# Half of a long convolution on VectorE, two taps a pass on TensorE, modulations turned in one piece, grouped heads' scores in F32

## The chip, the core and the metric

One NeuronCore of a Trainium2 chip runs the whole program. The metric is the device time of one execution in microseconds (us). Engines: PE is TensorE (PEld its weight loads), DVE VectorE, ACT ScalarE, POOL GpSimd, SP SyncE, which here only issues DMAs.

## The reference

One step of a two-layer diffusion backbone in F32, width 1024, on 128 context tokens and 512 latent tokens, which the program keeps side by side as 640 columns. Layer 0 mixes with convolutions, layer 1 with attention; each is followed by a SwiGLU network of width 2816. Cut to what the change touches:

```
m = silu(cvec) @ ada_w[l] + ada_b[l]              # 6 modulation vectors, for context and latents
h = rmsnorm(x) * (1 + scale) + shift
# layer 0
gate_b, gate_c, xa, ub = split(h @ w_in)
ya = gate_b * depthwise_conv(gate_c * xa, sc_w)   # 3 taps
z  = (ub + b)[:, :512] * sigmoid((ub + b)[:, 512:])
z  = depthwise_conv(z, cf_dw_w) + cf_dw_b         # 31 taps, 512 channels, context and latents apart
z  = silu(layernorm(z))
out = concat(ya, z) @ w_out + b_out
# layer 1: 8 grouped heads (2 key heads, 64 wide) and 8 latent-attention heads (96 wide)
s = q @ k.T;  p = softmax(s * scale);  o = p @ v  # latents see 128 + 512 cached and own keys
```

## The kernel before

Activations lie transposed, channels on partitions, tokens on columns; a 1024-wide vector is eight tiles of 128 partitions. A dense product `lin` (through `mm3`) takes three matmuls per tile: operands are split into a high and a low part in fp32r, and high·high, high·low and low·high are summed. Weights come as `raw` tiles of 512 KB, ACT makes the high part `whi`, DVE or POOL the low part `wlo`. An F32 matmul is one instruction, but two records in the trace.

`start` loads the tokens and the first 4 of 12 column groups of `ada_w[0]` (8 MB), multiplies them with two vectors (`cM`, 2 columns) into four 2-row strips of one PSUM tile (`ada`), and `ada_out` turns these strips into columns `mods`; then `modulate` makes `u` and `h`, first for columns 0 to 255 (GA), then for 256 to 639 (GB). The other groups are done by `ada_whole`, a generator whose steps (four matmuls `adaw` for one 128-row block; 16 steps while layer 0 mixes) are slipped in between other work.

`conv` computes `ub` for two channel blocks over GA, then GB, then for the other two blocks over both; the channel blocks `z0` to `z3` get the 31 taps. Context columns are done on DVE (`long_pro`, tile `acd`, 31 operations of 128x128 per block, the last in four 32-row pieces into `zp`). Latent columns are done on PE (`long_lat`): for each tap, 16 matmuls with 32x32 diagonal weights (`dg`) at all 4 x 4 positions of the array, into four PSUM tiles `tap`; `long_end` moves them back, with the bias. This stands between the products `gc`, `xa` and the product `gb` of the first half. `conv_norm` and `conv_out` follow.

In layer 1, `attn_q` makes the queries (tile `qf`, norm, rotary) and `store_k` and the cache loads the keys; for the grouped heads each is kept as a high and a low half on the two halves of the partitions (`qS`; `kS`, `kL`), so that one 128-row matmul with `kS` and one with `kL` give the score. `score` issues them per head and block of 128 queries: latents have 640 keys, in two column halves of 320 in two PSUM banks. The latent-attention heads use plain F32 (96 rows).

The order of instructions on each engine is set by the tile scheduler from the program order, priorities (`TAP_PRIO`, `BOUND_PRIO`) and buffer counts.

Of the kernel before, what the change touches and what calls it, by code (L numbers as in the profile page):

```python
# [9 lines left out]
F32 = mybir.dt.float32  # L10
# [14 lines left out]
KEYS = SEQ + PAST + LAT  # L25
FFN = 2816
# [27 lines left out]
TAP_BLOCK = 8  # L54
# [20 lines left out]
class Net:  # L75
# [266 lines left out]
    def params_in(self, b):  # L342

        nc, I, cst = self.nc, self.I, self.cst
        spec = [
# [6 lines left out]
             ("attn_q_norm", None, 1), ("attn_k_norm", None, 1)],  # L352
            [("conv_cf_dw_w", "o t (k p) -> (o t k) p", 124)],
        ]
        rows = self.cp.tile([P, P], F32, name=f"rows{b}")
        cols = cst.tile([P, P], F32, name=f"pcols{b}")
        dma = nc.gpsimd.dma_start if b else nc.scalar.dma_start
        r = 0
        for name, pat, n in spec[b]:
            if pat is None:  # L360
                for h in range(2):
                    dma(out=rows[r:r + 1, 64 * h:64 * h + 64], in_=I[name])
            elif pat.endswith("c"):
                dma(out=rows[r:r + n].rearrange("i (j c) -> i j c", c=32), in_=I[name].rearrange(pat, i=4, c=32))
# [67 lines left out]
    def ada_whole(self, l, groups):  # L432
# [16 lines left out]
        for i, (ch, k) in enumerate(todo):  # L449
            yield  # L450
            if k == 0:
                ps = self.ps("adaw")
            for j in range(4):
                nc.tensor.matmul(ps[32 * j:32 * j + 2, :], self.cM[:, k], ws[j], start=(k == 0), stop=(k == KD - 1))
            if i + 1 < len(todo):
                ws = load(i + 1)
            if k == KD - 1:
                self.ada_out(l, ch, ps, ("act",) * 4, self.ps)

    def ada_out(self, l, ch, ps, engines, alloc):  # L460

        row = self.arow.tile([P, 512], F32, name="arow", tag="arow", bufs=1)
        for j in range(4):
            r = slice(32 * j, 32 * j + 2)
            self.copy(engines[j], row[r], ps[r, :])
        for j in range(4):
            r = slice(32 * j, 32 * j + 2)
            pt = alloc("adat")
            for c in range(4):
                self.nc.tensor.transpose(pt[:, 2 * c:2 * c + 2], row[r, c * P:(c + 1) * P], self.ident[r, r])  # L470
            c0 = 4 * (ch + j)
            for v in range(2):
                self.nc.vector.tensor_tensor(self.mods[l][:, v, c0:c0 + 4], pt[:, :8].rearrange("p (c v) -> p v c", v=2)[:, v],
                                             self.par["ada_b"][:, 48 * l + c0:48 * l + c0 + 4], ALU.add)
# [198 lines left out]
    def start(self, X):  # L673
# [33 lines left out]
        ps = self.ps("ada0")  # L707
        for k in range(KD):
            for j in range(4):
                nc.tensor.matmul(ps[32 * j:32 * j + 2, :], self.cM[:, k], ada[k][j], start=(k == 0), stop=(k == KD - 1))  # L710
        self.ada_out(0, 0, ps, ("act", "dve") * 2, self.pp)
        H = [self.t5([P, 2, TOK], R32, name=f"h{k}") for k in range(KD)]
        for v in range(2):
            nc.vector.scalar_tensor_tensor(a[:, v], m[:, v, KD:2 * KD], 1.0, self.par["norm_pre"][:, 0:KD], ALU.add, ALU.mult)
        for (s, n), r in zip(AB, rb):
            for k in range(KD):
                us = {k: self.bt("u", n)}
                self.modulate([x[:, s:s + n] for x in X], us, r, s, n, (a, m[:, :, 0:KD]), H, k)
# [15 lines left out]
    def conv(self, H, M, ada):  # L734
# [31 lines left out]
        def diagonals():  # L766

            ds = []
            for t0 in range(0, CFK, TAP_BLOCK):
                n = 4 * min(TAP_BLOCK, CFK - t0)  # L770
                d = self.t5([P, 4 * TAP_BLOCK, 32], name="dg")
                nc.vector.tensor_tensor(d[:, :n], cw[:, 4 * t0:4 * t0 + n].unsqueeze(2).to_broadcast([P, n, 32]),
                                        self.eye32.unsqueeze(1).to_broadcast([P, n, 32]), ALU.mult)
# [3 lines left out]
        def long_lat(zs, ds):  # L777
# [4 lines left out]
            for t in range(CFK):  # L782
                d = ds[t // TAP_BLOCK][:, 4 * (t % TAP_BLOCK):4 * (t % TAP_BLOCK) + 4]
                for i in range(4):
                    r = slice(32 * i, 32 * i + 32)
                    for j in range(4):
                        nc.tensor.matmul(ps[i][32 * j:32 * j + 32, :LAT], d[r, j], zs[j][r, at + t:at + t + LAT],  # L787
                                         start=(t == 0), stop=(t == CFK - 1))
            return ps

        def long_pro(zs, made, zp):

            for j in range(4):
                while j not in made:
                    yield
                acc = t2("acd", SEQ, 2)
                col = lambda t: cw[:, 4 * t + j:4 * t + j + 1]
                nc.vector.tensor_scalar(acc, zs[j][:, :SEQ], col(0), None, ALU.mult)
                yield
                for t in range(1, CFK - 1):  # L800
                    nc.vector.scalar_tensor_tensor(acc, zs[j][:, t:t + SEQ], col(t), acc, ALU.mult, ALU.add)
                    yield
                t = CFK - 1
                for i in range(4):
                    r, o = slice(32 * i, 32 * i + 32), slice(32 * j, 32 * j + 32)
                    nc.vector.scalar_tensor_tensor(zp[o, i], zs[j][r, t:t + SEQ], col(t)[r], acc[r], ALU.mult, ALU.add)
                yield

        def long_end(zs, ps, zp):
            for i in range(4):  # L810
                b = par["conv_cf_dw_b"][:, i:i + 1]
                nc.scalar.activation(zs[i][:, SEQ:TOK], ps[i][:, :LAT], AF.Identity, bias=b)
                nc.scalar.activation(zs[i][:, :SEQ], zp[:, i], AF.Identity, bias=b)
# [10 lines left out]
        self.spawn(ada)  # L824
        made = set()
        zp = self.cp.tile([P, 4, SEQ], F32, name="zp")
        taps = self.rate(long_pro(zs, made, zp), TAP_STEPS)
        self.fine.append(taps)

        for hb, chs in ((0, GA), (0, GB), (1, AB)):  # L830
            b2 = self.block(w, 0, KD, 3 * SCW + 512 + 256 * hb, 256)
# [8 lines left out]
            for i in range(2):  # L840
# [7 lines left out]
                made.add(j)  # L848
# [74 lines left out]
    def conv_out(self, w, M, Z, zs, Y, bias, after, between):  # L923
# [4 lines left out]
        for ch in (GA, GB):  # L928
# [11 lines left out]
            for cb in range(4):  # L940
                raw = self.raw.tile([P, 4, 256], F32, name="raw", tag="raw", bufs=4)
                for j in range(4):
                    nc.sync.dma_start(out=raw[32 * j:32 * j + 32],
                                      in_=w[SCW + P * j:SCW + P * j + P, cb * 256:cb * 256 + 256]
                                      .rearrange("(i c) n -> c i n", c=32))
# [72 lines left out]
    def attn_q(self, H, ch, st):  # L1018
# [7 lines left out]
        for t in range(4):  # L1026
# [6 lines left out]
            f = tmp("qf")  # L1033
# [117 lines left out]
    def caches(self, t, st):  # L1151
# [12 lines left out]
        for g in range(2):  # L1164
            r, o = slice(64 * g, 64 * g + 64), slice(64 * (1 - g), 64 * (1 - g) + 64)
            kS, kL = st["kS"][g], st["kL"][g]
            nc.scalar.copy(kS[r, ks], ps[r, 0:P])
            nc.vector.tensor_tensor(kL[r, ks], ps[r, 0:P], fl(kS[r, ks]), ALU.subtract)
            nc.vector.tensor_copy(kS[o, ks], fl(kS[r, ks]))
            nc.vector.tensor_copy(kL[o, ks], fl(kL[r, ks]))  # L1170
# [6 lines left out]
    def attention(self, H, late, close_ph, close_tp):  # L1177
# [13 lines left out]
            qS=[self.t5([P, 2, TOK], R32, name=f"qS{t}") for t in range(4)],  # L1191
# [5 lines left out]
        if ATT_MIX:  # L1197
# [15 lines left out]
            kS=[T(gp, [P, KEYS], f"kS{g}", R32) for g in range(2)],  # L1213
            kL=[T(gp, [P, KEYS], f"kL{g}", R32) for g in range(2)],
# [36 lines left out]
    def heads(self, st, mp):  # L1251
# [92 lines left out]
        def score(h, qt, s):  # L1344
# [3 lines left out]
            for c, (k0, n) in enumerate(((0, SEQ),) if qt == 0 else ((SEQ, 320), (SEQ + 320, 320))):  # L1348
                o = s[:, c, :n]
                if h < 8:  # L1350
                    q, g = st["qS"][h // 2][:, h % 2, qs], h // 4
                    mm(o, q, st["kS"][g][:, k0:k0 + n], start=True, stop=False)
                    mm(o, q, st["kL"][g][:, k0:k0 + n], start=False, stop=True)
# [264 lines left out]
```

## Time and profile before

| | |
|---|---|
| time, median of 3 runs | 1697.18 us (1695.88 to 1697.71) |
| the profiled execution's own time | 1697.65 us |
| its span, first to last instruction | 1695.9 us |
| mean granted TensorE clock | 0.982 |
| busy: PE, DVE, ACT, POOL | 1632.8, 968.0, 655.1, 217.3 us |

The profile is of one execution. Busy time is the union of an engine's records; idle time of an engine that nobody waits for costs nothing. Numbers in the trace are us from the first instruction.

### The profile page before, as it was taken

The numbers are of one execution on the slowest core, as the hardware profiler recorded it, in microseconds if no ns is written. First come the engines' busy times: TensorE is split into PE (matmuls) and PEld (weight loads), VectorE is DVE, ScalarE is ACT, GpSimd is POOL, SyncE is SP. The second block draws the span as 40 slices with busy tenths as digits, with TensorE's granted clock in tenths as the row PEclk, the third lists the DMA queues.
The fourth block names the chain that finished last, engine by engine and source line by source line (L and its number), as shares of the span: only waits on it lengthen the run. The fifth ranks groups of instructions, "written<-read, shape, count | busy, mean of one in ns | idle before, by whom it ended". The sixth has DMA issues, their size and how long they took to land.

```text
span 1695.9 us, 28690 instructions
## 1 busy us (share of the span) xinstructions
PE 1632.8 (96%) x11569; PEld 1507.8 (89%) x11569; DVE 968.0 (57%) x2021; ACT 655.1 (39%) x1222; POOL 217.3 (13%) x239
## 2 busy tenths in 40 slices
PE   6999999989999999999988899999999999999998
PEld 2577599989999999999988786769899999999998
DVE  3767055888784735837988655455888102111246
ACT  2321135653222211234555576665643222212234
POOL 2000000110000000001202121111102333333301
PEclk9999999999999999999999799999999999999999
DMA  9764014347463433525344010025354222222232
GB/s 339 233 222 148 30 50 130 113 129 226 143 200 112 137 100 98 157 88 174 104 136 100 8 38 14 1 80 173 119 174 151 78 85 75 75 76 75 75 108 104
DMA packets 174406, 198.37 MB, mean 117 GB/s; under 512 B 18788, under 2 KB 152881, under 8 KB 174273
## 3 DMA queue, kind: packets, MB, share of 16 engines
q1 hardware_dynamic: 172224, 194.94, 36.8%
q8 instruction: 90, 1.47, 0.4%
q10 hardware_dynamic: 1600, 1.49, 0.3%
q14 instruction: 44, 0.35, 0.1%
q0 software_dynamic: 448, 0.11, 0.0%
HBM read 190.99 MB, written 5.52 MB: 116 GB/s over the span
## 4 chain that ended last, share of the span: by engine, by line
PE 86%; DVE 8%; DMA 3%; issue 2%; ACT 1%; DVEq 0%; POOL 0%; SPq 0%; ACTq 0%; POOLq 0%
PE pd L175 6%; PE pd L187 6%; PE pd L189 6%; PE pu L175 6%; PE pu L189 6%; PE pu L187 6%; PE pg L189 5%; PE pg L175 5%; PE pg L187 5%; PE av L1408 3%; PE tap L787 2%; PE s L1355 2%; PE po L187 2%; PE po L175 2%; PE po L189 2%; PE pT L975 2%
## 5 line engine op out<-in xcount | busy, mean ns | idle before, releaser
L134 ACT CAST whi<-raw 128x1024 fp32r<-128x1024 f32 (+1 forms) x260 | 264.1, 1018 | 445.1 <-PE pd L187 112.1
L139 DVE TENSOR_TENSOR wlo<-raw,whi 128x1024 fp32r<-128x1024 f32 (+3 forms) x219 | 258.5, 1182 | 137.7 <-ACT whi L134 133.3
L175 PE MATMUL pd<-hid,whi 128*128 128x320 f32 (+2 forms) x704 | 181.5, 310 | 0.0
L189 PE MATMUL pd<-hid,wlo 128*128 128x320 f32 (+2 forms) x704 | 181.4, 309 | 0.0
L187 PE MATMUL pd<-hid,whi 128*128 128x320 f32 (+2 forms) x704 | 181.2, 309 | 0.0
L623 DVE TENSOR_TENSOR sg<-pu,sg 128x320 f32<-128x320 f32 (+2 forms) x88 | 39.9, 483 | 247.0 <-PE pu L189 247.0
L175 PE MATMUL pu<-h,whi 128*128 128x320 f32 (+2 forms) x704 | 177.0, 311 | 0.0
L187 PE MATMUL pu<-h,whi 128*128 128x320 f32 (+2 forms) x704 | 176.7, 310 | 0.0
L187 PE MATMUL pg<-h,whi 128*128 128x320 f32 (+2 forms) x704 | 176.6, 310 | 0.0
L189 PE MATMUL pg<-h,wlo 128*128 128x320 f32 (+2 forms) x704 | 176.2, 310 | 0.0
L189 PE MATMUL pu<-h,wlo 128*128 128x320 f32 (+2 forms) x704 | 176.1, 310 | 0.0
L175 PE MATMUL pg<-h,whi 128*128 128x320 f32 (+2 forms) x704 | 176.1, 310 | 0.0
L139 POOL TENSOR_TENSOR wlo<-raw,whi 128x1024 fp32r<-128x1024 f32 (+1 forms) x48 | 112.0, 2339 | 234.7 <-ACT whi L134 234.7
L385 DVE SCALAR_TENSOR_TENSOR acc<-adaw,cT,acc 128x512 f32<-128x512 f32 x168 | 123.9, 790 | 11.2 <-DMA adaw<-in_ada_w 11.0
L187 PEld LDWEIGHTS pd<-hid,whi 128*128 128x128 f32 x704 | 123.5, 188 | 0.0
L189 PEld LDWEIGHTS pd<-hid,wlo 128*128 128x128 f32 x704 | 123.5, 188 | 0.0
L175 PEld LDWEIGHTS pd<-hid,whi 128*128 128x128 f32 x704 | 123.4, 188 | 0.0
L187 PEld LDWEIGHTS pu<-h,whi 128*128 128x128 f32 x704 | 122.9, 189 | 0.0
L175 PEld LDWEIGHTS pu<-h,whi 128*128 128x128 f32 x704 | 122.8, 189 | 0.0
L189 PEld LDWEIGHTS pg<-h,wlo 128*128 128x128 f32 x704 | 122.7, 189 | 0.0
L187 PEld LDWEIGHTS pg<-h,whi 128*128 128x128 f32 x704 | 122.7, 189 | 0.0
L189 PEld LDWEIGHTS pu<-h,wlo 128*128 128x128 f32 x704 | 122.7, 189 | 0.0
(457 smaller groups left out, 3065.3 us busy)
## 6 DMA issues: line engine op xcount, KB each, us to landing
raw<-in_ffn_w_gate SPq DMA_DIRECT2D x56, 512.0 KB, 3.9
raw<-in_ffn_w_up SPq DMA_DIRECT2D x56, 512.0 KB, 3.7
raw<-in_ffn_w_down SPq DMA_DIRECT2D x56, 512.0 KB, 3.4
adaw<-in_ada_w SPq DMA_DIRECT2D x96, 256.0 KB, 3.0
raw<-in_ada_w SPq DMA_DIRECT2D x36, 512.0 KB, 4.1
raw<-in_conv_w_in SPq DMA_DIRECT2D x24, 512.0 KB, 4.5
raw<-in_attn_w_in SPq DMA_DIRECT2D x16, 512.0 KB, 4.1
raw<-in_attn_w_out SPq DMA_DIRECT2D x16, 512.0 KB, 3.5
```

Of the source, the lines that this page charges most:

```text
L134: nc.scalar.copy(hi[:, :kt, :cols], rv)
L139: (self.nc.vector if (le or next(self.lo_mix)) == "dve" else self.nc.gpsimd).tensor_tensor(o, x, h, ALU.subtract)
L175: ins = [mm(o, whi, h, start=first, stop=False) for o, (h, l) in zip(outs, xs)]
L187: mm(o, whi, l, start=False, stop=False)
L189: mm(o, wlo, h, start=False, stop=last)
L385: ins = nc.vector.scalar_tensor_tensor(acc[v], w, self.cT[:, v, k:k + 1], acc[v], ALU.mult, ALU.add)
L623: nc.vector.tensor_tensor(tv(sg[i]), uv, tv(sg[i]), ALU.mult)
L787: nc.tensor.matmul(ps[i][32 * j:32 * j + 32, :LAT], d[r, j], zs[j][r, at + t:at + t + LAT], start=(t == 0), stop=(t == CFK - 1))
L975: self.nc.tensor.transpose(ps, src, self.ident[:m, :m])
L1355: mm(o, qM[(h - 8) // 2][:96, h % 2, qs], kM[h - 8][:96, k0:k0 + n], start=True, stop=True)
L1408: nc.tensor.matmul(av[o:o + 64, :w], value(u.h, k), u.pt[:, 0] if qt == 0 else u.pt[:, :, i], start=(i == 0), stop=(i == len(ks) - 1))
```

## The change

The long convolution of the latents is done on DVE for channel blocks 0 and 1 (31 operations of 128x512 each, the bias folded in), and on PE for blocks 2 and 3 only, two neighbouring taps in one pass: even taps sum up in rows 0 to 63 of the tap tiles, odd taps in rows 64 to 127, and `long_end` adds the two with DVE. `ada_out` copies all four strips as one 98-row tile and turns it with four transposes; the tile in PSUM is first set to zero. In `start` it and the first modulation get a higher priority. The other adaLN work starts with the second block (GB) instead of the first. Queries and keys of the grouped heads stay F32, without splitting; the two column halves of a score use partitions 0 to 63 and 64 to 127. The order of channels in the last convolution block changes with it: the loads of its parameters and of the output weights come in other pieces (not shown).

```diff
 def ada_whole(self, l, groups):
             if k == 0:
                 ps = self.ps("adaw")
+                nc.vector.memset(ps[:98], 0.0)
...
-                self.ada_out(l, ch, ps, ("act",) * 4, self.ps)
+                self.ada_out(l, ch, ps, ("act",), self.ps)
 def ada_out(self, l, ch, ps, engines, alloc):
-        for j in range(4):
-            r = slice(32 * j, 32 * j + 2)
-            self.copy(engines[j], row[r], ps[r, :])
-        for j in range(4):
...
+        n = 512 // len(engines)
+        for i, e in enumerate(engines):
+            self.copy(e, row[:98, i * n:i * n + n], ps[:98, i * n:i * n + n])
+        pt = alloc("adat")
+        for c in range(4):
+            self.nc.tensor.transpose(pt[:, c * P:c * P + 98], row[:98, c * P:(c + 1) * P], self.ident[:98, :98])
...
 def long_lat(zs, ds):
-            for t in range(CFK):
...
+            for t0 in range(0, CFK, 2):
                 for i in range(4):
                     r = slice(32 * i, 32 * i + 32)
+                    for t in range(t0, min(t0 + 2, CFK)):
+                        d = ds[t // TAP_BLOCK][:, t % TAP_BLOCK]
+                        for j in range(2):
+                            o = 64 * (t % 2) + 32 * j
+                            nc.tensor.matmul(ps[i][o:o + 32, :LAT], d[r, j], zs[2 + j][r, at + t:at + t + LAT],
+                                             start=(t < 2), stop=(t >= CFK - 2))
+        def long_dve(zs, made, zp):
+            for j, lat in ((0, 0), (1, 0), (0, 1), (1, 1), (2, 0), (3, 0)):
+                while (j, lat) not in made:
                     yield
...
+                    nc.vector.scalar_tensor_tensor(acc, zs[j][:, at + t:at + t + n], col(t), acc, ALU.mult, ALU.add)
...
 def long_end(zs, ps, zp):
-                nc.scalar.activation(zs[i][:, SEQ:TOK], ps[i][:, :LAT], AF.Identity, bias=b)
-                nc.scalar.activation(zs[i][:, :SEQ], zp[:, i], AF.Identity, bias=b)
+                nc.scalar.activation(z[r, SEQ:TOK], ps[i][:64, :LAT], AF.Identity, bias=b[r])
+                nc.vector.tensor_tensor(z[r, SEQ:TOK], ps[i][64:, :LAT], z[r, SEQ:TOK], ALU.add)
...
-        self.spawn(ada)
...
         for hb, chs in ((0, GA), (0, GB), (1, AB)):
+            if (hb, chs) == (0, GB):
+                self.spawn(ada)
 def attn_q
-                nc.scalar.copy(qS[r], f[r])
-                nc.vector.tensor_tensor(qS[o], f[r], fl(qS[r]), ALU.subtract)
+                nc.scalar.copy(sw[o], f[r])
 def store_k
-                nc.scalar.copy(kS[g][r, ks], kf[r, c:c + m])
-                nc.vector.tensor_tensor(kL[g][r, ks], kf[r, c:c + m], fl(kS[g][r, ks]), ALU.subtract)
-                nc.vector.tensor_copy(kS[g][o, ks], fl(kS[g][r, ks]))
-                nc.vector.tensor_copy(kL[g][o, ks], fl(kL[g][r, ks]))
+                self.keys_in(st, g, k0, raw["kf"][64 * g:64 * g + 64, c:c + m])
+    def keys_in(self, st, g, k0, x):
+        m = x.shape[1]
+        for a, b, r, c in ((k0, min(k0 + m, KH), 0, 0), (max(k0, KH), k0 + m, 64, KH - SEQ)):
+            if a < b:
+                self.copy(("act", "dve")[g], st["kF"][g][r:r + 64, a - c:b - c], x[:, a - k0:b - k0])
 def score(h, qt, s):
-                    mm(o, q, st["kS"][g][:, k0:k0 + n], start=True, stop=False)
-                    mm(o, q, st["kL"][g][:, k0:k0 + n], start=False, stop=True)
+                    r = slice(64 * c, 64 * c + 64)
+                    k0 = 0 if qt == 0 else SEQ
+                    mm(o, st["qF"][h // 2][r, (h + c) % 2, qs], st["kF"][h // 4][r, k0:k0 + n], start=True, stop=True)
```

On DVE, at the end of `start` in the kernel before (`arow` is the copied strip, `wlo` a weight split, `a` the scalars of the first modulation):

```order
L270 COPY arow<-ada_295 2x512
L473 TENSOR_TENSOR mods_98<-adat,pcols_159 128x4 x4
L139 TENSOR_TENSOR wlo<-raw,whi 128x1024
L270 COPY arow<-ada_295 2x512
L473 TENSOR_TENSOR mods_98<-adat,pcols_159 128x4 x2
L139 TENSOR_TENSOR wlo<-raw,whi 128x1024
L473 TENSOR_TENSOR mods_98<-adat,pcols_159 128x4 x2
L139 TENSOR_TENSOR wlo<-raw,whi 128x1024
L714 SCALAR_TENSOR_TENSOR a_294<-mods_98,pcols_159 128x8 x2
L139 TENSOR_TENSOR wlo<-raw,whi 128x1024
L506 SCALAR_TENSOR_TENSOR u<-x_108,a_294,spread 128x128 x2
```

The same place in the changed kernel:

```order
L272 COPY arow<-ada_301 98x256
L481 TENSOR_TENSOR mods_98<-adat,pcols_159 128x16 x2
L722 SCALAR_TENSOR_TENSOR a_300<-mods_98,pcols_159 128x8 x2
L513 SCALAR_TENSOR_TENSOR u<-x_108,a_300,spread 128x128 x2
L513 SCALAR_TENSOR_TENSOR u<-x_109,a_300,spread 128x128 x2
L513 SCALAR_TENSOR_TENSOR u<-x_110,a_300,spread 128x128 x2
L513 SCALAR_TENSOR_TENSOR u<-x_111,a_300,spread 128x128 x2
L141 TENSOR_TENSOR wlo<-raw,whi 128x1024 x2
L515 SCALAR_TENSOR_TENSOR h_347<-u,mods_98,h_347 128x128 x2
```

The four weight splits have moved from ahead of the first `u` to behind it.

On PE, in the taps of the changed kernel, the second of three such places (the adaLN products of one step stand one by one between tap matmuls); before there was one place of this kind:

```order
L800 MATMUL tap_1534<-z2_451,dg_1167 32x512
L461 MATMUL adaw_1363<-raw_1517,cM_100 2x512
L800 MATMUL tap_1534<-z3_452,dg_1167 32x512
L461 MATMUL adaw_1363<-raw_1517,cM_100 2x512
L800 MATMUL tap_1534<-z2_451,dg_1167 32x512
L461 MATMUL adaw_1363<-raw_1519,cM_100 2x512
L800 MATMUL tap_1534<-z3_452,dg_1167 32x512
L461 MATMUL adaw_1363<-raw_1519,cM_100 2x512
L800 MATMUL tap_1535<-z2_451,dg_1167 32x512
```

Behind the last of them and the rest of the taps, two more steps now stand among the products `gc` of the second half.

On DVE, at the end of the long convolution of the changed kernel (`acl` and `acd` hold its latents and context; L838 are the additions that empty the tap tiles):

```order
L824 SCALAR_TENSOR_TENSOR z_450<-z_450,pcols_187,acl 128x512
L820 SCALAR_TENSOR_TENSOR acd<-z_451,pcols_187,acd 128x128
L924 TENSOR_TENSOR lna<-z_449,z_450 128x256
L820 SCALAR_TENSOR_TENSOR acd<-z_451,pcols_187,acd 128x128 x11
L828 SCALAR_TENSOR_TENSOR zp<-z_451,pcols_187,acd 32x128 x4
L817 TENSOR_SCALAR acd<-z_452,pcols_187 128x128
L820 SCALAR_TENSOR_TENSOR acd<-z_452,pcols_187,acd 128x128 x29
L828 SCALAR_TENSOR_TENSOR zp<-z_452,pcols_187,acd 32x128 x4
L141 TENSOR_TENSOR wlo<-raw,whi 128x1024 x2
L838 TENSOR_TENSOR z_451<-tap,z_451 64x512
L838 TENSOR_TENSOR z_452<-tap,z_452 64x512
```

Before, ACT emptied the tap tiles and DVE had no part in it.

## Rows read from the trace of the kernel before

**Rows 1.** The page: the chain of work that ended last, by engine.
```profile
PE 86%; DVE 8%; DMA 3%; issue 2%; ACT 1%; DVEq 0%; POOL 0%; SPq 0%; ACTq 0%; POOLq 0%
```

**Rows 2.** Timeline of PE, start: start, duration, line, operation, records, idle before.
```profile
33.84 1.03 PE L710 MATMUL ada<-ada0w,cM 128*2 128x512 f32 x4 [0.33 <-DMA ada0w<-in_ada_w]
...
46.44 1.22 PE L175 MATMUL ub<-h,whi 128*128 128x256 f32 x4
...
51.35 1.03 PE L454 MATMUL adaw<-raw,cM 128*2 128x512 f32 x4
...
66.09 0.34 PE L175 MATMUL ub<-h,whi 128*128 128x384 f32 x1
```

**Rows 3.** Timeline of DVE, same stretch.
```profile
36.23 0.23 DVE L473 TENSOR_TENSOR mods<-adat,pcols 128x4 f32<-128x4 f32 x2
...
36.85 1.21 DVE L139 TENSOR_TENSOR wlo<-raw,whi 128x1024 fp32r<-128x1024 f32 x1
...
41.53 1.22 DVE L139 TENSOR_TENSOR wlo<-raw,whi 128x1024 fp32r<-128x1024 f32 x1
42.66 2.15 DVE L506 SCALAR_TENSOR_TENSOR u<-x,a,spread 128x128 f32<-128x128 f32 x8
```

**Rows 4.** Busy time by window: length, PE, PEld, DVE, ACT, POOL, clock, DMA.
```profile
40.00:45.00 5.00, 2.23 (x6) 0.19 (x8) 5.00 (x17) 2.54 (x8) 0.00 (x0) 0.50 0.78 248
```

**Rows 5.** The same view, from the second `ub` block to the taps' end.
```profile
65.00:209.00 144.00, 144.00 (x1611) 101.30 (x1609) 73.38 (x199) 25.43 (x38) 0.36 (x7) 0.98 0.45 144
```

**Rows 6.** Timeline of PE, taps.
```profile
164.21 23.68 PE L787 MATMUL tap<-z,dg 32*32 32x512 f32 x724
187.82 1.02 PE L454 MATMUL adaw<-raw,cM 128*2 128x512 f32 x2
188.77 1.04 PE L787 MATMUL tap<-z,dg 32*32 32x512 f32 x2
...
194.54 1.90 PE L787 MATMUL tap<-z,dg 32*32 32x512 f32 x34
196.37 0.41 PE L470 MATMUL adat<-con,arow 2*128 2x2 f32 x4
...
199.59 9.71 PE L787 MATMUL tap<-z,dg 32*32 32x512 f32 x198
209.74 0.39 PE L175 MATMUL gb<-h,whi 128*128 128x256 f32 x1 [0.44 <-ACT z L812]
```

**Rows 7.** Busy time by window, attention preparation, columns as in rows 4.
```profile
930.00:940.00 10.00, 3.85 (x14) 3.07 (x14) 7.51 (x32) 2.18 (x7) 0.76 (x2) 0.50 0.29 70
```

**Rows 8.** PE's waits, 815 to 950: total, times, longest.
```profile
PE spread L313 <- DVE rz L294: 5.9, 2, 3.6
```

**Rows 9.** DVE groups by form, 64 to 165: busy, mean ns, idle before.
```profile
L801 DVE SCALAR_TENSOR_TENSOR acd<-z,pcols,acd 128x128 f32<-128x128 f32 x116 | 33.2, 341 | 0.6
L764 DVE SCALAR_TENSOR_TENSOR sc<-pr,pcols,acs 128x512 f32<-128x512 f32 x1 | 0.7, 743 | 0.0
```

**Rows 10.** DVE groups by form, 815 to 950.
```profile
L1044 DVE TENSOR_TENSOR qS<-qf,qS 64x384 fp32r<-64x384 f32 x8 | 5.1, 633 | 0.3
L1044 DVE TENSOR_TENSOR qS<-qf,qS 64x256 fp32r<-64x256 f32 x8 | 3.6, 455 | 0.2
L1106 DVE CAST kL<-kL 64x384 fp32r<-64x384 f32 x2 | 1.4, 708 | 0.1
...
L1170 DVE CAST kL<-kL 64x128 fp32r<-64x128 f32 x2 | 0.4, 222 | 0.1
```

**Rows 11.** Timeline of PE: a unit of grouped heads, and one of the others.
```profile
952.98 0.41 PE L1352 MATMUL s<-kS,qS 128*128 128x320 f32 x1
...
953.67 0.71 PE L975 MATMUL pT<-con,prob 128*128 128x128 f32 x5
...
1090.60 1.34 PE L1355 MATMUL s<-kM,qM 96*128 96x320 f32 x4
1091.78 0.39 PE L1425 MATMUL rsum<-con,ribc 128*128 128x128 f32 x2
```

More of the change, by code (lines that the diff above doesn't have):

```diff
@@ L25 @@
 KEYS = SEQ + PAST + LAT
+KH = SEQ + (PAST + LAT) // 2
 FFN = 2816
@@ L52 @@
 TAP_STEPS = 2
-TAP_BLOCK = 8
+TAP_BLOCK = 16
 XCOPY = ('dve',) * 8
@@ L362, in params_in @@
                     dma(out=rows[r:r + 1, 64 * h:64 * h + 64], in_=I[name])
-            elif pat.endswith("c"):
-                dma(out=rows[r:r + n].rearrange("i (j c) -> i j c", c=32), in_=I[name].rearrange(pat, i=4, c=32))
+            elif pat == "c":
+                v = I[name][0]
+                dma(out=rows[r:r + 2], in_=v[0:256].rearrange("(k p) -> k p", p=P))
+                v = v[256:].rearrange("(j e h c) -> e h j c", j=2, e=2, h=2)
+                for e in range(2):
+                    dma(out=rows[r + 2 + e:r + 3 + e].rearrange("o (h j c) -> o h j c", h=2, j=2), in_=v[e:e + 1])
             else:
@@ L457, in ada_whole @@
             if k == KD - 1:
-                self.ada_out(l, ch, ps, ("act",) * 4, self.ps)
+                self.ada_out(l, ch, ps, ("act",), self.ps)
     def ada_out(self, l, ch, ps, engines, alloc):
         row = self.arow.tile([P, 512], F32, name="arow", tag="arow", bufs=1)
-        for j in range(4):
-            r = slice(32 * j, 32 * j + 2)
-            self.copy(engines[j], row[r], ps[r, :])
-        for j in range(4):
[L467 to L474, printed above, removed]
+        n = 512 // len(engines)
[4 more added lines that the diff above has]
+            self.nc.tensor.transpose(pt[:, c * P:c * P + 98], row[:98, c * P:(c + 1) * P], self.ident[:98, :98])
+        o = pt.rearrange("p (c j r) -> p j c r", c=4, r=32)
+        c0 = 4 * ch
+        for v in (0, 1):
+            m, b = self.mods[l][:, v, c0:c0 + 16], self.par["ada_b"][:, 48 * l + c0:48 * l + c0 + 16]
+            q = lambda x: x.rearrange("p (j c) -> p j c", c=4)
+            self.nc.vector.tensor_tensor(q(m), o[:, :, :, v], q(b), ALU.add)
     def scalars(self, l, i):
@@ L710, in start @@
                 nc.tensor.matmul(ps[32 * j:32 * j + 2, :], self.cM[:, k], ada[k][j], start=(k == 0), stop=(k == KD - 1))
-        self.ada_out(0, 0, ps, ("act", "dve") * 2, self.pp)
+        with self.tc.high_priority(BOUND_PRIO):
+            self.ada_out(0, 0, ps, ("act", "dve"), self.pp)
+            for v in range(2):
+                nc.vector.scalar_tensor_tensor(a[:, v], m[:, v, KD:2 * KD], 1.0, self.par["norm_pre"][:, 0:KD], ALU.add, ALU.mult)
         H = [self.t5([P, 2, TOK], R32, name=f"h{k}") for k in range(KD)]
-        for v in range(2):
-            nc.vector.scalar_tensor_tensor(a[:, v], m[:, v, KD:2 * KD], 1.0, self.par["norm_pre"][:, 0:KD], ALU.add, ALU.mult)
         for (s, n), r in zip(AB, rb):
@@ L717, in start @@
                 us = {k: self.bt("u", n)}
-                self.modulate([x[:, s:s + n] for x in X], us, r, s, n, (a, m[:, :, 0:KD]), H, k)
+                with self.tc.high_priority(BOUND_PRIO if s == 0 else 0):
+                    self.modulate([x[:, s:s + n] for x in X], us, r, s, n, (a, m[:, :, 0:KD]), H, k)
             if s == 0:
@@ L768, in diagonals @@
             ds = []
+            w2 = cw.rearrange("p (t j) -> p t j", j=4)[:, :, 2:4]
             for t0 in range(0, CFK, TAP_BLOCK):
[L770 to L773, printed above, removed]
+                n = min(TAP_BLOCK, CFK - t0)
+                d = self.t5([P, TAP_BLOCK, 2, 32], name="dg")
+                nc.vector.tensor_tensor(d[:, :n], w2[:, t0:t0 + n].unsqueeze(3).to_broadcast([P, n, 2, 32]),
+                                        self.eye32.unsqueeze(1).unsqueeze(1).to_broadcast([P, n, 2, 32]), ALU.mult)
                 ds.append(d)
@@ L823, in conv @@
         self.mix("dve")
-        self.spawn(ada)
         made = set()
-        zp = self.cp.tile([P, 4, SEQ], F32, name="zp")
-        taps = self.rate(long_pro(zs, made, zp), TAP_STEPS)
+        zp = self.cp.tile([P, 2, SEQ], F32, name="zp")
+        taps = self.rate(long_dve(zs, made, zp), TAP_STEPS)
         self.fine.append(taps)
         for hb, chs in ((0, GA), (0, GB), (1, AB)):
+            if (hb, chs) == (0, GB):
+                self.spawn(ada)
             b2 = self.block(w, 0, KD, 3 * SCW + 512 + 256 * hb, 256)
@@ L847, in conv @@
                     nc.vector.scalar_tensor_tensor(dst, src, cb[:, j:j + 1], g, ALU.add, ALU.mult)
-                made.add(j)
+                made.add((j, 0))
+                if chs != GA:
+                    made.add((j, 1))
         ds = diagonals()
@@ L941, in conv_out @@
                 raw = self.raw.tile([P, 4, 256], F32, name="raw", tag="raw", bufs=4)
[L942 to L945, printed above, removed]
+                wz, cols = w[SCW:], slice(cb * 256, cb * 256 + 256)
+                nc.sync.dma_start(out=raw[:, 0:2], in_=wz[0:256, cols].rearrange("(k p) n -> p k n", p=P))
+                for j in range(2):
+                    for h in range(2):
+                        o = 64 * h + 32 * j
+                        nc.sync.dma_start(out=raw[o:o + 32, 2:4], in_=wz[256 + P * j:256 + P * j + P, cols]
+                                          .rearrange("(e h c) n -> h c e n", e=2, h=2)[h])
                 hi, lo = self.gran(w, 4, 4, cb * 256, 256, raw=raw)
@@ L1032, in attn_q @@
             nc.scalar.activation(q, v, AF.Square)
-            f = tmp("qf")
+            f, sw = (st["qF"][t][:, i, s:s + n] for i in range(2))
             self.scale(QF[t], f, v, par["attn_q_norm"])
@@ L1164, in caches @@
         for g in range(2):
[L1165 to L1170, printed above, removed]
+            self.keys_in(st, g, SEQ, ps[64 * g:64 * g + 64, 0:P])
         for k in range(2):
@@ L1190, in attention @@
             qa=[self.t5([P, 2, TOK], R32, name=f"qa{k}") for k in range(3)],
-            qS=[self.t5([P, 2, TOK], R32, name=f"qS{t}") for t in range(4)],
+            qF=[self.t5([P, 2, TOK], name=f"qF{t}") for t in range(4)],
             wq=I["attn_w_q_b"][0].rearrange("(k p) (h d) -> k p h d", p=P, d=96),
@@ L1212, in attention @@
             qrt=[T(base, [P, TOK], f"qr{i}") for i in range(2)],
-            kS=[T(gp, [P, KEYS], f"kS{g}", R32) for g in range(2)],
-            kL=[T(gp, [P, KEYS], f"kL{g}", R32) for g in range(2)],
+            kF=[T(gp, [P, KH], f"kF{g}") for g in range(2)],
             Vg=[T(gp, [P, P], f"Vg{i}") for i in range(6)],
```

40 lines of the change are left out of this document (20 added, 20 removed), and 4 rows, old and new, of the table spec.

## Prediction

> **What bounds the kernel now.** First the page's chain of waits: 86% of the span is TensorE (PE), 8% VectorE (DVE), 3% DMA [rows 1]. So PE's queue is walked stage by stage, and a saving on another engine counts only where PE stands waiting for it. Four places touch the change.
>
> *Start.* PE finishes the last product of the first modulation at 33.84 + 1.03 = 34.87 and begins the first dense block, `ub`, at 46.44 [rows 2]. Between them lies DVE: four weight splits `wlo` of about 1.21 are mixed in, the first at 36.85, the last at 41.53, and the modulation `u` starts at 42.66 [rows 3]. From 40 to 45 PE is busy 2.23 of 5 us, and the granted clock is 0.50, the lower of its two levels [rows 4]. After that it is dense: from 65 to 209 it is busy 144 of 144 us [rows 5].
>
> *Taps.* The long convolution occupies PE from 164.21; the next dense block, `gb`, starts at 209.74: 45.5 us. Its first 724 records end at 187.82, so 32.6 ns a record. A tap is 16 matmuls of two records: 1.044 us. Four adaLN products then take turns with one or two tap matmuls until 194.54, 6.72 us in all: a lone matmul of either kind keeps PE for 0.95. From 199.59 on, 198 records take 9.71, or 49 ns each: part of it ran at half clock, after the small transposes that begin at 196.37 [rows 6].
>
> *Attention preparation.* PE is busy only 3.85 of the 10 us from 930 to 940, at clock 0.50, and DVE 7.51 [rows 7]. In the whole stretch PE's waits name DVE first: 5.9 us for `rz` [rows 8].
>
> *Scores.* PE does them back to back.
>
> **Part by part.**
>
> *First modulation as one tile.* Sixteen two-row transposes become four of 98 rows, four copies two, eight additions two, and in DVE's new order no split stands ahead of `u`. In the old order one round of copy, transposes and additions, the first, was done at 36.23 + 0.23 = 36.46, 1.6 after PE's end [rows 3]. The new one has one such round, with more columns in each piece, and the two scalars `a` behind it: `u` starts near 36.8 instead of 42.66, and the first `ub` near 38 instead of 46.44, as the adaLN products that stood before it are now spawned a block later. Against that, five splits now stand among `u` and `h` on DVE, and the first block GA is fed by DVE: 16 operations of 0.27 and five splits of 1.2 [rows 3] are 10.3, to which I add some 384-column operations and a PE that begins at the lower clock. I let GA end at 54; before, 66.09 [rows 2]: **12 us earlier**. Of this, 8 pairs of adaLN products (1.03 each [rows 2]), 8.2 us, are only put off. From there to the taps both orders hold 22 pairs, so the taps start near 152 instead of 164.
>
> *Two taps a pass.* 248 matmuls of two records at 32.6 ns: 16.2 us instead of 32.4. But the order puts three adaLN steps (four products each, one by one between tap matmuls) into the taps, where there was one. A step cost 6.72 less 0.3 for its taps: 6.4 [rows 6]; three cost 19.2. With 1.5 for the hand-overs, the stage lasts 37 instead of 45.5, and `gb` starts near 189, some 20 us earlier. Two more adaLN steps (four pairs, 4.1) and a turn of four transposes (0.4, as four small ones [rows 6]) now lie behind the taps, where nothing lay: 5 to 6 of debt. **Convolution: −20 + 6 = −14.** Bounds: −20, if nothing of the debt lands on PE's full stretches; −4 with the clock halved (below).
>
> In a step among dense blocks two pairs cost 2.1; between taps 6.4. The Trainium skill says (TensorEngine Tiling (Array Packing), Tiling Modes, Key Properties) that changing the tiling mode drains the engine. The trace agrees: 0.95 for a lone 32x32 tap between 128x2 products, 1.044 for sixteen together [rows 6].
>
> *Latents on DVE.* It adds 62 operations of 128x512. The nearest row, one of this shape and kind, is 0.743 [rows 9]. Those of 128x128 last 0.341, but 116 of them fill 33.2, 0.286 each [rows 9]: in a row they overlap by 0.055, so I take 0.69, and 43 us for the 62 (46 without any overlap). What goes with them, half the diagonals and of the 32-row ends, I leave uncounted. From 65 to 209 DVE is busy 73 of 144 [rows 5]; the new stretch, 54 to 189, has 135 for 73 + 43 = 116. What is late next, if this cover is gone, are the four additions that empty the tap accumulators: in DVE's order they stand behind all of the convolution and two splits, and `gb` needs those buffers. I put them at 184, the taps' end at 187.5: cost nothing, bound +5.
>
> *Attention: no splitting of queries and keys.* DVE loses 16 query subtractions (5.1 and 3.6 us) and nine groups of key splits, from 1.4 down to 0.4, in sum 7.5 [rows 10]; five copies of 0.22 or little more, as the last of these groups, come in: net 15. Some 7 of it (the eight wide subtractions, 5.1, and the wide key splits) stand ahead of the waits of 920 to 943, and I put 1 to 3 more in earlier, smaller waits; elsewhere PE is full, and nothing is won. **−8**; bounds 0 (the waits are for transfers or other DVE work) and −14.
>
> *Scores in F32.* Per head and latent block (32 units) four matmuls of 128 rows become two F32 ones of 64 rows, in the two halves of the rows. Four took 953.67 − 952.98 = 0.69; two F32 ones of 96 rows, one after the other, 1091.78 − 1090.60 = 1.18 [rows 11], so one 0.59. If the halves run side by side, a unit is 0.65 to 0.75: nothing. If not, 1.18: +0.5 x 32 = +16. The taps, where sixteen matmuls of 32 rows take hardly longer than one [rows 6], speak for side by side. I take +1; no row shows 64-row halves.
>
> The rest (loads of the parameters and of the output weights in other pieces, accumulators set to zero on DVE) goes at nothing: they run ahead, under dense PE, and would cost about 1 us an instance if they did not.
>
> **Sum**: −14 − 8 + 1 = −21. The profiled execution's own time, 1697.65, is 0.5 above the median of the runs, so the same shift gives **1676**.
>
> **Rivals.**
> 1. *The clock falls in the interrupted taps.* Three steps of lone matmuls are 20 us of thin work. Against it: the 6.72 us of the same kind did not bring it down; the fall came behind the small transposes that are gone from here. If it falls for half of that, +10: 1686.
> 2. *The attention gain stays hidden*: another DVE operation or a transfer holds the same wait. −14 + 1: 1684.
> 3. *The score halves run one after the other*: +16 in place of +1, 1691. The order of the units, each between 128-row transposes, and the rows' 0.59 speak for it, the taps against it.
> 4. *Each 64-row matmul starts only in an empty engine.* The four records of a unit of 96 rows are busy 1.34, but the next work starts after 1.18 [rows 11]: so 0.16 of overlap is lost at each of three boundaries, and I put as much again for weights loaded in the open. A unit is then 1.18 + 3 x 0.32 = 2.1, +1.45 x 32 = +46: 1721, slower. It decides from 1.34 a unit (0.69 + 21 / 32): above that nothing is left of the gain. The Trainium skill's rule of the drain (TensorEngine Tiling (Array Packing), Tiling Modes, Key Properties) speaks for it, as pT and the scores differ in mode; the trace agrees for taps and products only.
> 5. *DVE becomes the bound of the convolution*: 0.74 instead of 0.69, and splits queued behind the chains hold up blocks; +5 to +10: 1683.
> 6. *Interruptions cost less than 6.4*, or GA is fed faster, and the half clock of the start and the taps is gone: −6 to −10: 1668.
>
> **How the numbers follow.** The forecast, with its own range 1670 to 1681: 0.45. Rivals 1 to 6: 0.12, 0.11, 0.07, 0.05, 0.10, 0.10. The range, 1664 to 1691, leaves out rival 4, half of rival 3 and pairs of mishaps. What a measurement of this kernel can tell from no change is about 0.2%, 3.4 us. Slower by more: rival 4 and what sums of rivals 1, 3 and 5 reach: 0.07. Within: 0.06. Faster: 0.87.
>
> **What would show it.** In the changed trace: `u` at 36 to 38 and `ub` at 37 to 39; taps from 150 to 154, with three stretches of 6.5 of alternation at clock 1.00; `gb` at 187 to 191 without a wait for the additions; less PE idle time between 920 and 945 (less the shift), and a short wait for `rz`; a score unit at 0.6 to 0.8. The prediction would be wrong by a unit above 1.1, clock 0.50 in the taps, or DVE named in PE's waits through the convolution.

## The result and the profile after

| | before | after |
|---|---|---|
| median of 4 runs each | 1696.53 us | 1683.73 us (1682.58 to 1685.48) |
| ratio, 95% interval | | 0.9927 [0.9915, 0.9939] |
| profiled execution, own time (span) | 1697.65 (1695.9) | 1682.71 (1680.9) |

The kernel became faster by 12.8 us in the medians, 0.73% by the ratio, whose interval does not reach 1. The forecast was 1676, 21 us, with a range of 1664 to 1691: the direction was right, the size little more than half. Where the two traces drift apart is read from the first matmul of a few tiles. The first `gb` is 16.0 us earlier than before, the last `gb` 9.9, the first key product `pkf` of layer 1 10.5 (829.9 to 819.4), the last `rsum` of attention 16.6 (1143.1 to 1126.5). That is more than the medians give: the two profiled executions lie 14.9 apart, the first above its median and the second below, and 1.6 is lost again behind the last `rsum`, for a cause that no run shows.

The page's chain of the changed kernel; [rows 1] had 86% and 8%:

```profile
PE 89%; DVE 5%; DMA 3%; ACT 2%; issue 1%; POOL 0%; SPq 0%; DVEq 0%; ACTq 0%; POOLq 0%
```

Its timeline of PE at the start, which answers to [rows 2]:

```profile
33.72 1.03 PE L718 MATMUL ada<-ada0w,cM 128*2 128x512 f32 x4 [0.28 <-DMA ada0w<-in_ada_w]
35.22 0.85 PE L475 MATMUL adat<-con,arow 98*128 98x98 f32 x4 [0.47 <-ACT arow L270]
38.45 0.80 PE L177 MATMUL ub<-h,whi 128*128 128x256 f32 x2 [2.38 <-ACT h L514]
...
55.70 0.45 PE L177 MATMUL ub<-h,whi 128*128 128x384 f32 x1 [0.23 <-ACT sgm L867]
```

The first `ub` comes 8.0 us earlier, and the first block ends 10.4 earlier. In the taps (against [rows 6]) the three adaLN steps are plain to see, as `adaw` and `tap` in turn; each takes 6.7 us, and the stretches of taps alone get short:

```profile
154.15 9.03 PE L800 MATMUL tap<-z,dg 32*32 32x512 f32 x234
163.10 1.02 PE L461 MATMUL adaw<-raw,cM 128*2 128x512 f32 x2
164.05 1.04 PE L800 MATMUL tap<-z,dg 32*32 32x512 f32 x2
...
169.81 3.62 PE L800 MATMUL tap<-z,dg 32*32 32x512 f32 x98
173.36 1.02 PE L461 MATMUL adaw<-raw,cM 128*2 128x512 f32 x2
...
180.08 4.35 PE L800 MATMUL tap<-z,dg 32*32 32x512 f32 x114
184.35 1.02 PE L461 MATMUL adaw<-raw,cM 128*2 128x512 f32 x2
...
191.07 1.93 PE L800 MATMUL tap<-z,dg 32*32 32x512 f32 x32
193.78 0.39 PE L177 MATMUL gb<-h,whi 128*128 128x256 f32 x1 [0.77 <-DVE z L838]
```

DVE over the same stretch. Its convolution ends at 187.68 + 1.44 = 189.1, and the additions (L838) that free the tap buffers follow:

```profile
176.44 11.20 DVE L820 SCALAR_TENSOR_TENSOR acd<-z,pcols,acd 128x128 f32<-128x128 f32 x29
187.68 1.44 DVE L828 SCALAR_TENSOR_TENSOR zp<-z,pcols,acd 32x128 f32<-32x128 f32 x4
190.58 2.36 DVE L141 TENSOR_TENSOR wlo<-raw,whi 128x1024 fp32r<-128x1024 f32 x2 [1.46 <-ACT whi L136]
193.03 2.79 DVE L838 TENSOR_TENSOR z<-tap,z 64x512 f32<-64x512 f32 x4
```

So PE and DVE reach `gb` almost together, which no share of busy time shows. The wait of PE is 0.77.

In the attention preparation PE's waits on `rz` ([rows 8]) are gone. From 815 to 950 it is idle for 12.2 us instead of 19.4, as the busy time in these windows shows (columns as in [rows 4]; the kernel before, then the changed one):

```profile
815.00:950.00 135.00, 115.58 (x741) 110.81 (x740) 116.12 (x348) 66.46 (x137) 20.04 (x21) 0.90 0.37 101
815.00:950.00 135.00, 122.76 (x789) 109.38 (x788) 108.35 (x319) 73.65 (x162) 24.89 (x34) 0.95 0.34 93
```

What is left lies mostly earlier, on the second chunk's `h` and on `kfa`, which DVE computes behind eight operations of that chunk. PE first, then DVE:

```profile
843.08 0.38 PE L177 MATMUL pcf<-h,whi 128*128 128x256 f32 x1 [1.72 <-ACT cf0a L1101]
...
854.08 0.44 PE L177 MATMUL pkf<-h,whi 128*128 128x384 f32 x1 [1.80 <-ACT h L514]
856.63 0.33 PE L1008 MATMUL nk<-con,kfa 128*128 128x128 f32 x1 [2.11 <-DVE kfa L1119]
858.24 0.69 PE L177 MATMUL pvf<-h,whi 128*128 128x384 f32 x1 [1.28 <-ACT qaf L263]
```

```profile
851.90 4.28 DVE L513 SCALAR_TENSOR_TENSOR y<-x,a,spread 128x384 f32<-128x384 f32 x8
856.11 0.47 DVE L1119 SCALAR_TENSOR_TENSOR kfa<-kfa,pcols,rbk 128x256 f32<-128x256 f32 x1
```

The waits for `h` and, before `pvf`, for `qaf` are new. The one for `kfa` is not: in the kernel before it stood behind the same eight operations, and PE waited 1.58 for it (PE, then DVE):

```profile
868.11 0.33 PE L975 MATMUL nk<-con,kfa 128*128 128x128 f32 x1 [1.58 <-DVE kfa L1088]
```

```profile
863.37 4.29 DVE L506 SCALAR_TENSOR_TENSOR y<-x,a,spread 128x384 f32<-128x384 f32 x8 [1.17 <-PE spread L313]
```

A unit of scores (against [rows 11]) is 939.24 − 938.50 = 0.74:

```profile
938.50 0.81 PE L1377 MATMUL s<-kF,qF 64*128 64x320 f32 x4
939.24 0.41 PE L177 MATMUL mqr<-qa,whi 128*128 128x320 f32 x1
```

### The profile page after: what moved, and what is told of

Same layout as the page of the kernel before. It is cut to its first block, busy times and chain, and to the rows that moved or that the text cites. A ratio compares the mean times of both kernels' runs of the same rounds, so it can differ in the third digit from the quotient of the medians.

```text
span 1680.9 us, 27646 instructions
## 1 busy us (share of the span) xinstructions
PE 1627.4 (97%) x11037; PEld 1482.5 (88%) x11037; DVE 994.8 (59%) x2028; ACT 649.2 (39%) x1210; POOL 220.8 (13%) x245
## 4 chain that ended last, share of the span: by engine, by line
PE 89%; DVE 5%; DMA 3%; ACT 2%; issue 1%; POOL 0%; SPq 0%; DVEq 0%; ACTq 0%; POOLq 0%
PE pd L177 6%; PE pd L189 6%; PE pd L191 6%; PE pu L177 6%; PE pu L189 6%; PE pu L191 6%; PE pg L189 6%; PE pg L191 6%; PE pg L177 6%; PE av L1432 3%; PE pT L1008 2%; PE po L189 2%; PE po L177 2%; PE adaw L461 2%; PE po L191 2%; PE s L1379 2%
## 5 line engine op out<-in xcount | busy, mean ns | idle before, releaser
L177 PEld LDWEIGHTS pg<-h,whi 128*128 128x128 f32 x704 | 122.6, 189 | 0.0
L189 PEld LDWEIGHTS pg<-h,whi 128*128 128x128 f32 x704 | 122.5, 189 | 0.0
```

The costliest lines, as they stand in the source:

```text
L177: ins = [mm(o, whi, h, start=first, stop=False) for o, (h, l) in zip(outs, xs)]
L189: mm(o, whi, l, start=False, stop=False)
```

## Experiments

Line numbers in each trace are those of that kernel. "Changed" is the changed kernel, 1683.73.

**The attention edits taken out (e1), and alone in the kernel before (e9).**

```diff
-                    mm(o, st["qF"][h // 2][r, (h + c) % 2, qs], st["kF"][h // 4][r, k0:k0 + n], start=True, stop=True)
+                    mm(o, q, st["kS"][g][:, k0:k0 + n], start=True, stop=False)
+                    mm(o, q, st["kL"][g][:, k0:k0 + n], start=False, stop=True)
```

(with `attn_q`, `store_k` and the caches as before; e9 is the reverse, in the kernel before.)

> The changed kernel with the attention of the kernel before (queries and keys split, four matmuls a score unit); convolution and adaLN parts stay changed. Theory (two separate gains, read from the milestones of the two traces: 10.5 us are won until the first feed-forward network, 6 more between the key products and the last score): about 6 us slower than the changed kernel, 1690, and 7 faster than before. Rival (the attention edits gain nothing by themselves, the later milestones only move with what stands ahead): within 2 us of the changed kernel, 1684.

> The kernel before with the attention edits alone (queries and keys unsplit, F32 scores in the two row halves). Theory (what the run without them showed: 3.4 us): 1692 to 1693 against 1695.6. Rival (the milestones of the two traces: 6 us from the key products to the last score): 1689 to 1690.

Measured: e1 1687.08 (ratio to before 0.9948 [0.9936, 0.9961]), e9 1691.29 (0.9972 [0.9962, 0.9982]; before in that set 1696.64). So the attention edits are worth 5 us alone and 3.4 beside the others, the convolution and adaLN edits 8.6; both lie between what the two theories said of them, and the parts add up to the whole within the intervals. An interval reaches about 2 us to either side, so 5 and 3.4 are not told apart. PE's idle time from 815 to 950 goes the same way: 18.1 in e1 and 12.2 in e9, as in the changed kernel:

```profile
815.00:950.00 135.00, 116.91 (x738) 110.72 (x739) 114.79 (x338) 68.72 (x149) 23.17 (x28) 0.90 0.34 94
815.00:950.00 135.00, 122.81 (x805) 112.96 (x804) 111.01 (x323) 72.69 (x156) 21.78 (x30) 0.95 0.38 101
```

**DVE's load in the preparation put back (e11).**

```diff
                 nc.scalar.copy(sw[o], f[r])
+                nc.vector.tensor_tensor(st["idle"][o, s:s + n], f[r], f[r], ALU.subtract)
...
+        for _ in range(3):
+            self.nc.vector.tensor_copy(e, x)
```

> The changed kernel with VectorE's load in the attention preparation put back: 16 subtractions of the sizes of the removed ones and 24 copies of the keys' pieces, all into a tile that nobody reads; scores stay F32. Theory (the attention edits gain by VectorE's relief in the preparation): the 3 to 5 us of the edits are lost, 1687 to 1689. Rival (they gain in the scores and their hand-overs): within 1 us of the changed kernel, 1683 to 1685.

Measured: 1693.55, 10 slower than the changed kernel (to before 0.9991 [0.9981, 1.0002]). That is more than the 3 to 5 of the theory. In its timeline of PE a score's wait for ACT's `qaf` (3.57 in the kernel before), which the changed kernel had lost, is back with 4.38, the next one has grown from 2.27 to 3.23, and the first `mqr` comes at 941.3 instead of 928.4:

```profile
923.55 0.79 PE L1382 MATMUL s<-kF,qF 64*128 64x128 f32 x2 [4.38 <-ACT qaf L263]
927.58 1.44 PE L1382 MATMUL s<-kF,qF 64*128 64x320 f32 x4 [3.23 <-ACT prob L1412]
```

From 815 to 950 PE is idle for 20.4, against 12.2 in the changed kernel: 8 of the 10.

```profile
815.00:950.00 135.00, 114.62 (x720) 104.37 (x721) 115.32 (x345) 69.53 (x151) 22.32 (x30) 0.91 0.34 92
```

So with the scores as in the changed kernel and the load back, nothing of the attention edits' gain is left: it hangs on the relief of DVE. What the relief is worth e11 cannot say, as the load costs two to three times what its removal gave. Operations whose result nobody needs stand elsewhere in DVE's order than the real ones did; whether that is the reason is not shown.

**Both score halves in the same rows (e3).** The keys are stored in these rows too.

```diff
-                    r = slice(64 * c, 64 * c + 64)
+                    r = slice(0, 64)
```

> The changed kernel, but both column halves of a grouped head's score use partitions 0 to 63 (keys stored there, one query copy), so the two F32 matmuls share their rows; all else as in the changed kernel. Theory (in the changed kernel the two halves run side by side: 0.74 us a unit, where one alone needs about 0.59): a unit takes 1.2, 0.45 more, times 32: 14 us slower, 1698. Rival (row position plays no part, the unit is short for another reason): 0.74 a unit again, 1684.

Measured: 1703.86, 20 slower than the changed kernel, and slower than before (1.0045 [1.003, 1.006]).

```profile
946.41 1.34 PE L1376 MATMUL s<-kF,qF 64*128 64x320 f32 x4
947.68 0.55 PE L1008 MATMUL pT<-con,prob 128*128 128x128 f32 x3
```

A unit is 1.27 instead of 0.74, times 32 is 17 of the 20; the other 3 are not accounted for. In two row halves the two F32 matmuls do run side by side; without that the whole change would have been a loss.

**The old turning of the modulations (e8).** `ada_out`, and the priorities in `start`, as before; the spawn stays late.

```diff
-            self.ada_out(0, 0, ps, ("act", "dve"), self.pp)
+        self.ada_out(0, 0, ps, ("act", "dve") * 2, self.pp)
```

> The changed kernel with the modulations turned in sixteen two-row transposes again, four copies and eight additions, and the first modulation without its priority; spawn of the adaLN steps unchanged. Theory (at the start only the chain through this turn counts): u starts at 42 instead of 36.6, the first block ends 4 to 5 us later, and small transposes behind the taps cost 1 more: 1688 to 1690. Rival (the first block is fed by VectorE's splits anyway, so the early u gains little): within 2 us of the changed kernel, 1684 to 1686.

Measured: 1688.22, 4.5 slower than the changed kernel, as the theory said: PE waits 4.30 for `u`, and the first `ub` stands at 44.07, not 38.45.

**The adaLN steps kept out of the taps (e2).**

```diff
-            while self.bg_due >= 1:
-                self.bg_due -= 1
-                self.tick(self.bg)
+        with self.tc.high_priority(self.bg_prio):
+            while self.bg_due >= 1:
+                self.bg_due -= 1
+                self.tick(self.bg)
```

`bg_prio` is `BOUND_PRIO`, but 0 from the taps to the end of `conv`.

> The changed kernel, but adaLN steps that are issued after the taps in program order get no priority, so no step stands between tap matmuls: the three steps move behind the taps. Theory A (the prediction's: a step costs 6.4 us between taps and 2.1 among dense blocks, and VectorE is done in time): taps last about 20 us instead of 38, gb starts at 175, the three steps come back for 6.4: 13 us faster, 1671. Theory B (VectorE's own convolution, done at 189 in the changed kernel, with the four additions queued behind it, is a second bound only just behind PE): gb still starts at 190 or later, PE waits some 15 us for the additions, and the three steps are paid again behind them: 1684 to 1690, not faster.

Measured: 1687.20 (0.9945 [0.9933, 0.9958]), 3.5 slower than the changed kernel: theory B. PE is through with the taps and two steps behind them (16 records) at 173, and then it stands:

```profile
154.00 17.57 PE L802 MATMUL tap<-z,dg 32*32 32x512 f32 x496
171.50 1.90 PE L463 MATMUL adaw<-raw,cM 128*2 128x512 f32 x16
190.82 0.58 PE L178 MATMUL gb<-h,whi 128*128 128x256 f32 x1 [17.42 <-DVE z L840]
```

`gb` starts 3.0 earlier than in the changed kernel, but that does not last: one more step than there lies among the later products, and behind the wait PE runs at a mean granted clock of 0.64 until 196, where the changed kernel has 1.00.

**DVE's order freed, with the steps held (e6) and without (e10).** The contexts of blocks 2 and 3 run as two alternating chains, and the last 17 taps of block 1's latents come behind the additions.

```diff
+            yield from long_dve(zs, made, zp, ((0, 0), (1, 0), (0, 1)))
+            a, b = (long_dve(zs, made, zp, ((j, 0),)) for j in (2, 3))
+            for _ in a:
+                next(b, None)
+                yield
+            yield from b
...
+        last = long_dve(zs, made, zp, ((1, 1),))
...
+                        nc.vector.scalar_tensor_tensor(k1, zs[2][:, SEQ:SEQ + CFK], 0.0, cw.rearrange("p (t j) -> p t j", j=4)[:, :, 1], ALU.mult, ALU.add)
```

Of `last`, taps 0 to 13 are issued ahead of `long_end`, the rest behind it. The last line makes these wait: its coefficients get 0 times an element that the additions write.

> As the held version, and VectorE's order is changed so that the additions do not wait for the whole convolution: the contexts of channel blocks 2 and 3 run as two alternating chains ahead of the latents of block 1, and the last 17 taps of block 1's latents come behind the additions (an extra 128x31 operation makes them wait). If theory A or B holds, PE no longer waits: gb at about 176, 1671 to 1674. Theory B says so for this run alone and not for the held one; theory A for both. If neither holds (the steps cost as much elsewhere), 1684.

> The freed order of VectorE alone: the additions no longer wait for the whole convolution, but the three adaLN steps stay between the taps (the fourth corner beside the changed kernel, the held and the freed-and-held version). Theory (two bounds lie one behind the other: PE's interrupted taps end at 192 to 193, VectorE's convolution at 189): taking the second away alone gains nothing, gb starts at 193, 1682 to 1685. Rival (the gain of 17 us of the freed version came from VectorE's order alone): 1670 or less.

Measured: e6 1666.01 (0.9821 [0.9808, 0.9835]), e10 1683.97 (0.9936 [0.9922, 0.995]). Neither edit gains alone (+3.5 and +0.2 against the changed kernel), both together gain 17.7: two bounds, one right behind the other, as theory B said. In e6 `gb` follows the taps and the first steps at once, while DVE, from 172 on, adds first and finishes the latents behind it:

```profile
154.12 17.62 PE L802 MATMUL tap<-z,dg 32*32 32x512 f32 x496
171.67 1.90 PE L463 MATMUL adaw<-raw,cM 128*2 128x512 f32 x16
173.50 0.38 PE L178 MATMUL gb<-h,whi 128*128 128x256 f32 x1
```

```profile
172.24 2.64 DVE L846 TENSOR_TENSOR z<-tap,z 64x512 f32<-64x512 f32 x4 [2.03 <-ACT z L845]
174.91 0.21 DVE L825 SCALAR_TENSOR_TENSOR k<-z,pcols 128x31 f32<-128x31 f32 x1
175.16 6.26 DVE L828 SCALAR_TENSOR_TENSOR acl<-z,k,acl 128x512 f32<-128x512 f32 x8
```

e6 is the fastest version found: 30 us less than before, and faster than expected, as `gb` comes at 173.5 and not at 176. The two steps behind the taps took 1.90, or 0.95 each, in one unbroken run; a step in two pairs among dense blocks was reckoned at 2.1, and one between taps takes 6.7. So the steps do not only move in e6, they get cheaper.

**The early spawn put back (e4).**

```diff
+        self.spawn(ada)
         made = set()
...
-            if (hb, chs) == (0, GB):
-                self.spawn(ada)
```

> The changed kernel with the adaLN steps spawned ahead of the first block, as in the kernel before; nothing else undone. 15 of 16 steps then stand among dense blocks before the taps, one in the taps, none behind. Theory (a step costs 2.1 us among dense blocks and 6.4 between taps, and VectorE's convolution, done at 189, is the next bound): taps start 8 us later, last 26 instead of 39, gb starts at 190 to 193 and nothing is owed behind it: 6 to 8 faster than the changed kernel, 1676 to 1678. Rival (at the start the adaLN loads hold up the weight loads, which the later spawn was for): the first block is late by more than the 8 us, 1682 or more.

Measured: 1692.00 (0.9973 [0.9963, 0.9983]), slower by 8, and by neither account: the time is one that the rival allows, but its cause is not to be seen. The start is in order (`ub` at 39.91, behind a modulation product that itself ended 1.5 later), and the taps begin at 164.08. But the turn of the second modulation group now falls into them, and its copy `arow` stands on ACT behind two activations that wait for DVE's `zp`:

```profile
196.24 0.40 ACT L840 ACTIVATE z<-zp,pcols 128x128 f32<-128x128 f32 x1 [31.30 <-DVE zp L828]
196.97 0.40 ACT L840 ACTIVATE z<-zp,pcols 128x128 f32<-128x128 f32 x1 [0.34 <-DVE zp L828]
197.28 0.57 ACT L270 COPY arow<-adaw 98x512 f32<-98x512 f32 x1
```

PE stood 16.96 us before the transposes in the midst of the taps. It is the same bound as in e2, reached through ACT's queue.

**DVE nearly idle in the taps (e7).** The length of the taps alone is compared. DVE is busy for 3.35 us there, all of them ahead of 158.

> The held version with the work of VectorE in the taps left out: no latents of channel block 1 and only the first and last tap of the contexts of blocks 2 and 3 (so its output is not the reference's). Only the length of the taps counts. Theory (VectorE's stream over the same tiles slows the tap matmuls): 248 matmuls take about 16.2 us, as their steady rate of 30.8 ns a record in the kernel before, with VectorE idle, says. Rival (two taps in a pass read the same tile at neighbouring columns and are slower by themselves): 17.5 again, as in the held run.

Measured, in one execution: 16.9 us from the first tap to the next product (154.10 to 170.98), against 17.5 in e2. DVE's stream costs 0.6, half of what theory said. The rival does not fill the rest: the first 14 us of the taps hold 435 records in the kernel before, 436 in e7 and 420 in e2, so with DVE nearly idle two taps in a pass go as fast as one. The expected 16.2 is 496 records at the 32.6 ns of [rows 6] (the 30.8 named would give 15.3); the 0.7 that e7 lies above it is in the last records and at the stretch's end.

## Why the prediction was right or wrong

**Start: right, a little too early.** `u` at 36.60 (36.8 forecast), `ub` at 38.45 (38), the end of GA at 55.70 (54), the taps at 154.15 (152). The two early estimates held. The end of GA, read at the next block's first product, was 1.7 late, but most of that is one of the 22 adaLN pairs, which stands ahead of that product (54.44 to 55.47): GA's own products end at 54.5. e8 prices the turn with its priorities at 4.5, near the 12 less the 8.2 put off.

**Taps: the steps right, the taps themselves mis-sized.** Three steps cost 6.7 each with their taps, as said, and the clock was 1.00 throughout, so rival 1 fell. But the term "248 matmuls at 32.6 ns a record: 16.2" was too small: the 239 matmuls outside the steps took 8.95 + 3.55 + 4.27 + 1.9 = 18.7, where 15.6 was reckoned. Of these 3.1, about 1.8 go with the cutting into four: in one piece (e2) 248 take 17.5, so 239 would take 16.9. DVE's stream makes 0.6 (e7), and the other 0.7 lie in the last records and at the stretch's end. The stage took 39.6, not 37.

**Debt: right.** `gb` was 16.0 ahead at its first and 9.9 at its last matmul: 6.

**DVE as cover: the verdict right by luck.** The additions were put at 184 and the taps' end at 187.5: cost nothing. DVE was through with its convolution at 189.1 and with the two splits behind it at 192.9, and PE waited no more than 0.77 (0.44 before) only because the taps were late too, at 193.0. Had they ended as forecast and `gb` been ready at 189, PE would have waited some 2 to 5 us, an estimate from the `gb` of e2 (190.82) and of this trace (193.78): the bound "+5". Two sizes were off. The last 40 context operations took 0.38 to 0.39 each (the 29 of block 3 0.386), where [rows 9] had 0.286: in the kernel before two chains alternated there, here each operation waits for the one ahead. That is 4 us. And the first of the two splits waited 1.46 for ACT. The text also took "+5" for the whole risk. e2 shows what lay behind it: with the steps out of the way, PE stands 17 us for DVE. So the 4.3 between a step's 6.4 and 2.1 could not be had back by moving the products alone.

**Attention: right in kind and near in size, but part of it was taken back.** The waits from 920 to 943 did go (e11 shows that this hangs on DVE's relief). PE's idle time from 815 to 950 fell by 7.2 against the kernel before (in e9 too) and by 5.9 against e1, where −8 was put: the waits ahead of that stretch did not shrink, as 1.80 for `h` and 1.28 for `qaf` are new and the one for `kfa` grew from 1.58 to 2.11. Of this gain the scores take 1.6 back. That leaves 5.6 alone and 4.3 beside the other edits, against 5 and 3.4 measured.

**Scores: right.** 0.74 a unit against 0.69: +1.6, with +1 forecast; rivals 3 and 4 are out, and e3 shows that 3 would have cost 17 to 20. The Trainium skill (TensorEngine Tiling (Array Packing), Tiling Modes, Key Properties) says that different tiles can run their matmuls in parallel; the trace agrees, 0.74 against 1.27. The Trainium skill's rule of the drain at a change of mode (the same section) costs little here: 0.74 is 0.15 above the 0.59 that one matmul of 96 rows takes [rows 11].

Altogether: convolution and adaLN 8.6 instead of 14, as the taps started 2.1 late and the stage took 2.6 more (the traces, whose executions lie further apart than the medians, have 9.9 of the 14); attention and scores 3.4 instead of 7.

## What to carry to other kernels

Before costing a shorter stage, write down when each engine is through with its share: here PE's path and DVE's ended within 4 us of each other, so neither of two edits alone gained anything, and both together gained 18. Look at what stands in front of the instruction that frees a buffer on its own queue, not only at that engine's total. And a removed load pays only until the next wait in the same stage, so count the gaps around it, not the instructions removed.

## What was not expected of the hardware

- A chain of 128x128 operations on DVE, each reading the last one's result, took 0.386 us each (29 in 11.20, above). Two such chains in turn (they start at 69.27 and 69.46) took 0.265, as this group of the kernel before shows:

```profile
69.66 10.32 DVE L801 SCALAR_TENSOR_TENSOR acd<-z,pcols,acd 128x128 f32<-128x128 f32 x39
```

- Two F32 matmuls of 64 rows by 320 columns in the two row halves took 0.74 us together, and 1.27 in the same half.
- 248 tap matmuls took 17.5 us in one stretch, 16.9 with DVE nearly idle.
- Eight adaLN products in one run took 1.90 us (171.67 in e6), as long as two that stand singly between taps (0.95 each, from 163.10 to 164.05 in the changed kernel).
